# Five of eight experts in two passes with at most 64 tokens, other buffer counts, and a branch

## The chip, the cores and the metric

The kernel runs on one core of a Trainium2 chip. The metric is the device time of one execution in microseconds (us); the time shown is the median of several runs. The engines of the core work beside one another, each in its own order, and wait for one another by semaphores: TensorE (PE for its matmuls, PEld for its weight loads), VectorE (DVE), ScalarE (ACT), GpSimd (POOL) and SyncE (SP), which here issues the transfers from memory.

## The reference

Two layers over 256 tokens of 2048 float32 values. The even layer mixes by pooling and stick-breaking attention and then has a dense SwiGLU network of width 5632; the odd layer mixes by a gated unit and then sends each token to two of eight experts:

```python
DN_ALPHA = (2.0 * DEPTH) ** 0.25

def moe_swiglu(x, w_router, w_gu, w_down):
    logits = jnp.dot(xt, w_router, preferred_element_type=jnp.float32)
    top_vals, top_idx = lax.top_k(logits, TOP_K)                # 2 of 8
    top_w = jax.nn.softmax(top_vals, axis=-1)
    gates = jnp.sum(jax.nn.one_hot(top_idx, N_EXPERTS) * top_w[..., None], axis=1)
    y = jnp.zeros(xt.shape, jnp.float32)
    for e in range(N_EXPERTS):
        y = y + gates[:, e:e + 1] * swiglu(xt, w_gu[e], w_down[e])
    return y

def swiglu(x, w_gu, w_down):
    gate, up = jnp.split(x @ w_gu, 2, axis=-1)                  # 2048 -> 2 x 1408
    return (jax.nn.silu(gate) * up) @ w_down                    # 1408 -> 2048

h = layer_norm(DN_ALPHA * h + mixed @ odd_w_out, odd_ln1_g, odd_ln1_b)
h = layer_norm(DN_ALPHA * h + moe_swiglu(h, odd_router, odd_moe_w_gu, odd_moe_w_down), odd_ln2_g, odd_ln2_b)
```

## The kernel before

Stages, by the trace: the even mixer and its output projection to about 311 us, the dense network to 1047 us (11 column blocks, gate and up, then down), the odd mixer, its projection and the router to about 1340 us, eight experts to 2154.5 us, the final normalisation and output to 2174.2 us.

Products of float32 values are made from two parts each. A value is rounded to a shorter type (`fp32r`), which is its high part, and the remainder is what the rounding lost. `mm3` (lines 117 to 119) adds three products to one accumulator: high times high, high times the weights' remainder, remainder times the weights' high part.

All weights come by `load` (lines 97 to 110). A load brings PIECE = 4 row chunks of 128 x 512 (1 MB; 0.75 MB for narrower column blocks) into a buffer `raw` on SyncE's queue (line 106), ScalarE casts it to the high part `wh` (line 107), VectorE subtracts to get the remainder `wl` (line 108). There are five `raw` buffers and four pairs of `wh` and `wl`. A `raw` buffer is free for the next transfer when its split is done, a pair when the last matmul that reads it is. Before the experts, every block of loaded weights serves two token tiles of 128; the loop over pieces goes through both tiles.

An expert works on its own tokens only. `gather` compares each token's place in the expert's list with the numbers 1 to 128 (VectorE, line 819), which gives a one-hot matrix `Dt` for each token tile; a product with the tokens (line 837) brings up to 128 tokens into the columns of `xe`, high part and remainder, for two experts in one go. `slots` (line 848) turns `Dt` and reads the gates. `expert_up` makes gate and up in three column blocks (512, 512 and 384), each from four loads of four chunks, and the SwiGLU, whose product is transposed (line 181) and split. `expert_down` runs through four blocks of 512 columns of three loads (4, 4 and 3 chunks), scales by the gate and scatters back with `Dt` (lines 900 and 901), and adds to `h` (line 234). An expert is 24 loads of 1 MB and 12 of 0.75 MB. In the down part of experts 1, 3 and 5 the next pair is gathered, a quarter in each block.

If an expert has more than 128 tokens, a loop at the end (lines 728 to 751) runs all experts again for the rest; it stands behind a branch on the value `most`, and isn't run with these inputs.

The order of the instructions within each engine is found ahead of time by a planner, from its own estimates of durations; both arms of a branch are planned as units of their own. There is no barrier at the entry of an arm. At its end every engine waits for its own work, SyncE for all its transfers to land, before it jumps on.

## Time and profile before

| | |
|---|---|
| median of 3 runs | 2174.91 us (2174.14 to 2175.73) |
| the profiled execution: time, span | 2175.96 us, 2174.2 us |
| mean granted TensorE clock | 0.994 |
| PE busy | 2140.0 us (98%) |
| PEld busy | 1781.5 us (82%) |
| DVE busy | 1456.7 us (67%) |
| ACT busy | 1146.6 us (53%) |
| POOL busy | 1.6 us |
| DMA | mean 247 GB/s, 537.80 MB |
| end of experts 0 to 7 | 1458.8, 1562.4, 1658.4, 1762.8, 1859.5, 1963.2, 2059.3, 2154.5 us |

Busy times are of the whole span; the stages differ, so they have to be read by stretches. The experts' ends are those of their last scatter (line 901). Line numbers are those of the kernel before. The rows of a view of windows give, for a stretch (us from the start), its length, the busy us and the count of instructions of PE, PEld, DVE, ACT and POOL, the mean granted clock as a share of full speed (PEclk), the mean busy share of the 16 DMA engines, and the GB/s moved. A row of a group of instructions gives line, engine, operation, the tile written and those read, and their shapes; x is a count. "issue" and engine names with a q (SPq, DVEq) are the sequencer of that engine: what it spends waiting, loading registers or branching.

### The profile page before, as it was taken

Reading aid. Unit: us, or ns where it says so; the run is one execution under the profiler, and the core shown is the slowest. Engines: PE = TensorE matmul, PEld = TensorE weight load, DVE = VectorE, ACT = ScalarE, POOL = GpSimd, SP = SyncE. Lnnn points to the kernel's source line nnn. Section 1 sums busy time; section 2 is a strip of 40 time slices with the busy share of each in tenths; the row PEclk is TensorE's granted clock in tenths of the full one; section 3 lists DMA queues with packets and bytes.
Section 4 is the critical chain, followed back from the end, with each engine's and each line's share of the span. In section 5 each row is a group of like instructions: output and inputs, shape, how many; then the busy total and the mean of one; then the engine's idle time right before and its main releaser. Section 6 shows DMA issues by size and latency. Waiting matters only on the chain.

```text
span 2174.2 us, 24450 instructions
## 1 busy us (share of the span) xinstructions
PE 2140.0 (98%) x9955; PEld 1781.5 (82%) x9956; DVE 1456.7 (67%) x1225; ACT 1146.6 (53%) x962; POOL 1.6 (0%) x6
## 2 busy tenths in 40 slices
PE   9999999999999999999999999999999999999996
PEld 7888888888888888888788887888888888888884
DVE  5443566554454644556676546898889888888988
ACT  5444355343333433343644335766766767676764
POOL 0000000000000000000000000000000000000000
PEclk9999999999999999999999999999999999999998
DMA  8544645555454554545544643899989999998995
GB/s 347 217 147 145 233 180 208 211 194 191 157 215 172 213 189 169 204 169 218 213 182 166 235 155 117 320 352 357 340 331 367 347 336 342 346 352 322 371 351 213
DMA packets 82198, 537.80 MB, mean 247 GB/s; under 512 B 9504, under 2 KB 10656, under 8 KB 28192
## 3 DMA queue, kind: packets, MB, share of 16 engines
q1 hardware_dynamic: 82080, 536.18, 66.3%
q8 instruction: 80, 1.31, 0.2%
q14 instruction: 38, 0.31, 0.0%
HBM read 534.04 MB, written 2.10 MB: 247 GB/s over the span
## 4 chain that ended last, share of the span: by engine, by line
PE 93%; DVE 3%; ACT 2%; DMA 1%; issue 0%; SPq 0%; DVEq 0%; ACTq 0%
PE acc L118 29%; PE acc L119 28%; PE acc L117 28%; PE ps L181 2%; DVE wl L108 1%; PE ps L837 1%; ACT wh L107 1%; PE ps L900 1%; DMA raw<-in_odd_moe_down_dram 1%; DMA raw<-in_even_w_in_dram 1%; PE ps L901 1%; ACT lnT L259 0%; PE ps L575 0%; PE acc L135 0%; PE acc L629 0%
## 5 line engine op out<-in xcount | busy, mean ns | idle before, releaser
L108 DVE TENSOR_TENSOR wl<-raw,wh 128x2048 fp32r<-128x2048 f32 (+2 forms) x519 | 1121.3, 2178 | 391.5 <-ACT wh L107 390.8
L107 ACT CAST wh<-raw 128x2048 fp32r<-128x2048 f32 (+2 forms) x519 | 935.4, 1824 | 442.1 <-PE acc L119 399.3
L118 PE MATMUL acc<-wl,xh 128*128 128x512 f32 x928 | 363.3, 392 | 1.1 <-DVE wl L108 1.1
L117 PE MATMUL acc<-wh,xh 128*128 128x512 f32 x928 | 361.8, 390 | 0.1
L119 PE MATMUL acc<-wh,xl 128*128 128x512 f32 x928 | 361.6, 390 | 0.0
L118 PE MATMUL acc<-wl,xe 128*128 128x512 f32 (+1 forms) x752 | 280.7, 373 | 0.1
L119 PE MATMUL acc<-wh,xe 128*128 128x512 f32 (+1 forms) x752 | 279.4, 372 | 0.0
L117 PE MATMUL acc<-wh,xe 128*128 128x512 f32 (+1 forms) x752 | 278.6, 371 | 0.5 <-ACT wh L107 0.5
L118 PE MATMUL acc<-wl,hTh 128*128 128x512 f32 x704 | 277.3, 394 | 1.1 <-DVE wl L108 1.0
L119 PE MATMUL acc<-wh,hTl 128*128 128x512 f32 x704 | 276.1, 392 | 0.0
L117 PE MATMUL acc<-wh,hTh 128*128 128x512 f32 x704 | 274.8, 391 | 0.0
L118 PEld LDWEIGHTS acc<-wl,xh 128*128 128x128 f32 x928 | 174.4, 188 | 37.0 <-DVE wl L108 1.5
L117 PEld LDWEIGHTS acc<-wh,xh 128*128 128x128 f32 x928 | 174.2, 188 | 37.1 <-ACT xh L174 0.5
L119 PEld LDWEIGHTS acc<-wh,xl 128*128 128x128 f32 x928 | 174.4, 188 | 35.7 <-DVE xl L175 0.2
L118 PEld LDWEIGHTS acc<-wl,xe 128*128 128x128 f32 x752 | 141.2, 188 | 21.2 <-DVE wl L108 1.8
L117 PEld LDWEIGHTS acc<-wh,xe 128*128 128x128 f32 x752 | 141.2, 188 | 20.7 <-ACT wh L107 0.8
L118 PEld LDWEIGHTS acc<-wl,hTh 128*128 128x128 f32 x704 | 132.3, 188 | 30.3 <-DVE wl L108 3.5
L119 PEld LDWEIGHTS acc<-wh,xe 128*128 128x128 f32 x752 | 141.3, 188 | 19.0
L117 PEld LDWEIGHTS acc<-wh,hTh 128*128 128x128 f32 x704 | 132.3, 188 | 28.3
L119 PEld LDWEIGHTS acc<-wh,hTl 128*128 128x128 f32 x704 | 132.4, 188 | 26.4
L174 ACT CAST hTh<-ps 128x512 fp32r<-128x512 f32 (+1 forms) x46 | 26.2, 569 | 180.4 <-PE ps L181 180.4
L117 PE MATMUL acc<-wh,x0h 128*128 128x512 f32 x256 | 104.1, 409 | 2.5 <-ACT wh L107 2.5
(201 smaller groups left out, 1820.0 us busy)
## 6 DMA issues: line engine op xcount, KB each, us to landing
raw<-in_odd_moe_gu_dram SPq DMA_DIRECT2D x128, 1024.0 KB, 6.9
raw<-in_even_ffn_gu_dram SPq DMA_DIRECT2D x88, 1024.0 KB, 4.8
raw<-in_odd_moe_down_dram SPq DMA_DIRECT2D x64, 1024.0 KB, 7.0
raw<-in_odd_moe_gu_dram SPq DMA_DIRECT2D x64, 768.0 KB, 6.1
raw<-in_even_ffn_down_dram SPq DMA_DIRECT2D x44, 1024.0 KB, 4.8
raw<-in_odd_w_in_dram SPq DMA_DIRECT2D x32, 1024.0 KB, 4.8
raw<-in_even_w_in_dram SPq DMA_DIRECT2D x30, 1024.0 KB, 5.0
raw<-in_odd_moe_down_dram SPq DMA_DIRECT2D x32, 768.0 KB, 6.8
```

Source lines behind the costliest of these rows:

```text
L107: nc.scalar.copy(wh, raw)
L108: self.wl_ins = nc.vector.tensor_tensor(wl, raw, wh.bitcast(F32), ALU.subtract)
L117: mm(acc, xh, wh, start=first, stop=False)
L118: mm(acc, xh, wl, start=False, stop=False)
L119: mm(acc, xl, wh, start=False, stop=last)
L174: self.nc.scalar.copy(hi, src)
L181: self.nc.tensor.transpose(ps[:, j * P:(j + 1) * P], src[:, j * P:(j + 1) * P], self.ident)
L837: mm(o, xtok[t, c // 8][part][:, cs], Dt[t].rearrange("p a b -> p (a b)"), start=j == 0 and t == 0, stop=t == 1, skip_group_check=True)
L900: nc.tensor.matmul(ps, DT[:, t, :], yh, start=True, stop=False)
L901: nc.tensor.matmul(ps, DT[:, t, :], yl, start=False, stop=True)
```

## The change

The eight experts are no longer all alike and no longer in the order 0 to 7.

- Expert 0 runs as before, but its tokens are gathered alone. While it runs, a new function `order` sorts the other seven by whether they have more than SLIM = 64 tokens: those with more come first. The sort is 23 small operations of VectorE, and the seven expert numbers are loaded into registers of SyncE, so that weights are addressed by a register.
- The first FATS = 2 of the sorted seven run as before, in three passes with up to 128 tokens ("fat" experts). For them the next pair is gathered in expert 0's down part.
- The last five stand behind a branch on `full`, the count of experts among the seven with more than 64 tokens. If at most two have more, the new arm runs them as "slim" experts. If not, the other arm runs them as before.
- A slim expert holds at most 64 tokens. `gather_slim` puts the tokens' high parts into columns 0 to 63 of a 128-column operand and their remainders into columns 64 to 127. One matmul with the weights' high part then makes two of the three products, and a second one with the weights' remainder a third (and a fourth, remainder times remainder): two passes instead of three. `fold` adds rows 64 to 127 of the accumulator to rows 0 to 63: ScalarE copies the accumulator, and a product with a shifted identity is added to it. In the down part the hidden values stand in the same way, and the scatter, with `Dt` in both halves, does the adding.
- In the slim arm two experts are gathered at its start, three more in the second one's down part. The first EARLY = 2 loads of the first of the five experts are made ahead of the branch and used by either arm.
- There are seven `raw` buffers instead of five, and three split pairs instead of four, in the whole kernel.
- In the last down projection of the dense network the order changes from all four column blocks of token tile 0, then all of tile 1, to block 0 of tile 0 and of tile 1, then blocks 1 to 3 of tile 0, then blocks 1 to 3 of tile 1.
- The final scales and biases (G, B) are still loaded behind all experts' loads in the program, which is now behind the branch.

```diff
+SLIM = 64
+EARLY = 2
+FATS = 2
+REST = NEXP - 1
...
-        nc.sync.dma_start(raw, src)
+        self.issued = nc.sync.dma_start(raw, src)
...
-                order = [(t, n) for t in range(NT) for n in range(NCB)] if last else \
-                        [(t, n) for n in range(NCB) for t in range(NT)]
+                order = [(t, n) for n in range(NCB) for t in range(NT)]
+                if last:
+                    order.sort(key=lambda k: k[1] > 0 and 1 + k[0])
...
-                    if last and (t, n) in ((1, 0), (1, NCB - 1)):
+                    if last and (t, n) in ((1, 1), (1, NCB - 1)):
...
+        self.fold = pm.tile([P, P], F32R, tag="fold", name="fold", bufs=1)
+        nc.gpsimd.memset(self.fold[:, SLIM:].bitcast(F32), 0.0)
+        nc.gpsimd.tensor_copy(self.fold[:, :SLIM], self.ident[:, SLIM:])
...
-        gat = self.gather(xtok, [pos1[t][:, 0:2] for t in range(NT)], gg, 0, 0)
+        gat = self.gather(xtok, [pos1[t][:, 0:1] for t in range(NT)], gg, 0, 0, num=1)
...
+        many = pm.tile([P, REST], F32, tag="many", name="many", bufs=1)
+        nc.vector.tensor_scalar(many, cnt[:, 1:NEXP], float(SLIM), None, ALU.is_gt)
+        ids, posP, full = [], [], pm.tile([P, 1], I32, tag="full", name="full", bufs=1)
+        def gather(k, num):
+            return self.gather(xtok, [posP[t][:, k:k + num] for t in range(NT)], gg, NEXP + k, 0, num=num)
+        def gather_slim(k, num):
+            return self.gather_slim(xtok, [posP[t][:, k:k + num] for t in range(NT)], num)
+        def prepare():
+            order = self.order(many, pos1, gates, gate_cols, posP, full)
+            ins, v = nc.values_load_multi_w_load_instructions(
+                order[0:1, :], engines=[mybir.EngineType.SP], min_val=1, max_val=REST)
+            self.after(ins[0], self.issued)
+            ids.extend(v)
+        hT = self.expert_up(0, gat, 0, first, prepare)
+        gat[4]()
+        cur, gat = gat, gather(0, FATS)
+        gat[4]()
+        self.expert_down(0, cur, 0, hT, True, None, gat[3])
+        for p in range(FATS):
+            hT = self.expert_up(ids[p], gat, p)
+            self.expert_down(ids[p], gat, p, hT, False, None)
+        full_v = nc.values_load(full[0:1, 0:1], min_val=0, max_val=REST)
+        src = i["odd_moe_gu"][ids[FATS], 0]
+        early = [self.load(src[k]) for k in range(EARLY)]
+        with tc.If(full_v < FATS + 1) as slim:
+            at = 0
+            A, step = gather_slim(FATS, 2)
+            for q in range(4):
+                step(q)
+            for k in range(FATS, REST):
+                ahead = partial(gather_slim, k + 1, REST - k - 1) if k == FATS + 1 else None
+                nxt = self.slim_expert(ids[k], k - FATS - at, A, gg, NEXP + k, fstats if k == REST - 1 else None,
+                                       early if k == FATS else None, ahead)
+                if nxt is not None:
+                    A, at = nxt, 2
+        with slim.Else():
+            for k in range(FATS, REST, 2):
+                num = min(2, REST - k)
+                gat = gather(k, num)
                 gat[4]()
-            step = None
-            if e % 2 and e + 1 < NEXP:
-                gat = self.gather(xtok, [pos1[t][:, e + 1:e + 3] for t in range(NT)], gg, e + 1, 0)
-                gat[4]()
-                step = gat[3]
-            self.expert_down(e, cur, e % 2, hT, e == 0, fstats if e == NEXP - 1 else None, step)
+                for q in range(4):
+                    gat[3](q)
+                for p in range(num):
+                    hT = self.expert_up(ids[k + p], gat, p, early=None if k + p > FATS else early)
+                    self.expert_down(ids[k + p], gat, p, hT, False, fstats if k + p == REST - 1 else None)
...
+    def order(self, hv, pos1, gates, gate_cols, posP, full):
...
+        self.after(v.tensor_reduce(H, hv, AX.X, ALU.add), self.wl_ins)
+        v.tensor_copy(full, H)
+        v.tensor_tensor(sq, rows(hv), square(C_LOWER), ALU.mult)
+        v.tensor_reduce(rank, sq, AX.X, ALU.add)
+        v.scalar_tensor_tensor(a, e7, H, rank, ALU.add, ALU.subtract)
+        v.tensor_tensor(b, rank, a, ALU.subtract)
+        v.tensor_tensor(b, b, hv, ALU.mult)
+        v.tensor_tensor(a, a, b, ALU.add)
+        v.tensor_tensor(perm, rows(a), square(C_PLACE), ALU.is_equal)
+        v.tensor_scalar(b, e7, 1.0, None, ALU.add)
+        v.tensor_tensor(sq, perm, rows(b), ALU.mult)
+        v.tensor_reduce(b, sq, AX.X, ALU.add)
+        v.tensor_copy(ids, b)
+        for t in range(NT):
+            g = tile("gateP", [P, R], bufs=2)
+            x = tile("posP", [P, R], bufs=2)
+            for dst, src in ((x, pos1[t]), (g, gates[t])):
+                v.tensor_tensor(sq, perm, rows(src[:, 1:NEXP]), ALU.mult)
+                v.tensor_reduce(dst, sq, AX.X, ALU.add)
+            gate_cols(t, g, 2 * NEXP, R)
+            posP.append(x)
+        return ids
...
+    def gather_slim(self, xtok, pos, num):
+        nc, pm = self.nc, self.pm
+        mm = nc.tensor.matmul
+        slots = self.iota1[:, :SLIM].unsqueeze(1).to_broadcast([P, 2, SLIM])
+        d4 = []
+        for t in range(NT):
+            d = pm.tile([P, num, 2, SLIM], F32R, tag="Dt", name="d4", bufs=2)
+            for p in range(num):
+                nc.vector.tensor_scalar(d[:, p], slots, pos[t][:, p:p + 1], None, ALU.is_equal)
+            d4.append(d)
+        A, units = {}, {}
+        per = 4 // num if num < 3 else 1
+        w = num * SLIM
+        hold = 8 // num if num < 3 else 2
+        def quarter(q):
+            for c in range(4 * q, 4 * q + 4, per):
+                if c % hold == 0:
+                    units[0] = self.unit("xs", shape=[P, hold, num, 2, SLIM])
+                ps = self.ps()
+                for j in range(per):
+                    cs = slice((c + j) % 8 * P, ((c + j) % 8 + 1) * P)
+                    for part in range(2):
+                        o = ps[:, (2 * j + part) * w:(2 * j + part + 1) * w]
+                        for t in range(NT):
+                            mm(o, xtok[t, (c + j) // 8][part][:, cs], d4[t][:, :, 0, :],
+                               start=j == 0 and part == 0 and t == 0, stop=t == 1, skip_group_check=True)
+                for j in range(per):
+                    u = units[0][:, (c + j) % hold]
+                    nc.scalar.copy(u, ps[:, 2 * j * w:2 * (j + 1) * w].rearrange("p (a e s) -> p e a s", a=2, e=num))
+                    A[c + j] = u
+        return (A, d4), quarter
...
+    def slim_expert(self, e, p, gat, gg, col, stats, early, ahead):
+        nc, i, pm = self.nc, self.i, self.pm
+        mm = nc.tensor.matmul
+        A, d4 = gat
+        def two(groups, lhs, w):
+            acc = self.acc()
+            n, k0 = sum(g[2] for g in groups), 0
+            for wh, wl, kc in groups:
+                for j in range(kc):
+                    mm(acc[:, :w], lhs(k0 + j), wh[:, j, :], start=k0 + j == 0, stop=False)
+                    mm(acc[:, :w], lhs(k0 + j), wl[:, j, :], start=False, stop=k0 + j == n - 1)
+                k0 += kc
+            return acc
+        def fold(acc, w):
+            c = self.pln.tile([P, CB], F32R, tag="lnT", name="low")
+            nc.scalar.copy(c[:, :w], acc[:, :w])
+            mm(acc[:, :w], self.fold, c[:, :w], start=False, stop=True, skip_group_check=True)
+        hT = []
+        for b, w in enumerate(EXP_W):
+            accs = [two(self.up_loads(e, b, u, early),
+                        lambda k: A[k][:, p], w) for u in range(2)]
+            for acc in accs:
+                fold(acc, w)
+            nch = w // P
+            s = self.pln.tile([P, CB], F32, tag="lnT", name="silu")
+            nc.scalar.activation(s[:, :w], accs[0][:, :w], AF.Silu)
+            nc.vector.tensor_tensor(s[:, :w], s[:, :w], accs[1][:, :w], ALU.mult)
+            pv = self.transpose4(s, nch)[:, :w].rearrange("p (c t) -> p c t", c=nch)[:, :, :SLIM]
+            h = pm.tile([P, 4, 2, SLIM], F32R, tag="hTh", name="hT2", bufs=3)
+            nc.scalar.copy(h[:, :nch, 0, :], pv)
+            nc.vector.tensor_tensor(h[:, :nch, 1, :], pv, h[:, :nch, 0, :].bitcast(F32), ALU.subtract)
+            hT.append(h)
+        DT, gs = self.slots([d4[t][:, p] for t in range(NT)], gg, col)
+        nxt, step = (None, None) if ahead is None else ahead()
+        for n in range(NCB):
+            if step is not None:
+                step(n)
+            acc = two(self.down_loads(e, n), lambda k: hT[k // 4][:, k % 4], CB)
+            self.scatter(acc, DT, gs, n, False, stats)
+        return nxt
...
-                groups = self.loads(i["odd_moe_gu"][e, b * 2 + u] if b < 2 else i["odd_moe_gu2"][e, u], w)
-                accs.append(self.block(groups, lhs, 0, w))
+                accs.append(self.block(self.up_loads(e, b, u, early), lhs, 0, w))
             hT.append(self.swiglu(pm, accs[0], accs[1], w, w // P, "m"))
+            if then is not None and b == 0:
+                then()
...
+    def up_loads(self, e, b, u, early):
+        src = i["odd_moe_gu"][e, b * 2 + u] if b < 2 else i["odd_moe_gu2"][e, u]
+        if early is None or b or u:
+            return self.loads(src, EXP_W[b])
+        return early + [self.load(src[k]) for k in range(EARLY, src.shape[0])]
...
-        self.praw = e(self.pool("raw", 5))
-        self.pw = e(self.pool("w", 4))
+        self.praw = e(self.pool("raw", 7))
+        self.pw = e(self.pool("w", 3))
```

## Rows read from the trace of the kernel before

**Rows 1.** Windows by stage: length, busy (count) of five engines, PEclk, DMA share, GB/s.

```profile
0.00:1340.00 1340.00, 1332.34 (x6081) 1093.65 (x6083) 742.97 (x681) 568.23 (x506) 1.61 (x6) 1.00 0.53 196
1459.00:2154.50 695.50, 692.90 (x3318) 590.04 (x3317) 595.91 (x396) 489.07 (x373) 0.00 (x0) 1.00 0.92 343
```

**Rows 2.** Windows, the same columns: expert 2, and the last five experts.

```profile
1562.40:1658.40 96.00, 96.00 (x451) 82.10 (x451) 83.83 (x54) 66.75 (x46) 0.00 (x0) 1.00 0.93 349
1658.40:2154.50 496.10, 493.52 (x2357) 419.54 (x2357) 424.87 (x282) 346.55 (x263) 0.00 (x0) 1.00 0.91 342
```

**Rows 3.** Waits of SyncE's queue: waiting line, releaser; us in all, times, longest.

```profile
SPq L106 <- DVE wl L108: 1785.4, 494, 20.5
```

**Rows 4.** Timeline of PE: start, duration, engine, line, operation, shapes, type, count.

```profile
1499.74 0.39 PE L118 MATMUL acc<-wl,xe 128*128 128x512 f32 x1
1499.97 0.39 PE L119 MATMUL acc<-wh,xe 128*128 128x512 f32 x1
1500.20 0.33 PE L118 MATMUL acc<-wl,xe 128*128 128x384 f32 x1
1500.37 0.34 PE L119 MATMUL acc<-wh,xe 128*128 128x384 f32 x1
...
1551.78 1.10 PE L837 MATMUL ps<-Dt,xtl 128*128 128x256 f32 x8
```

**Rows 5.** Groups by form, 1460 to 2060 us: busy, mean ns, idle before.

```profile
L108 DVE TENSOR_TENSOR wl<-raw,wh 128x2048 fp32r<-128x2048 f32 x144 | 325.5, 2288 | 51.0 <-ACT wh L107 50.8
L108 DVE TENSOR_TENSOR wl<-raw,wh 128x1536 fp32r<-128x1536 f32 x72 | 124.3, 1754 | 13.6 <-ACT wh L107 13.2
```

**Rows 6.** Timeline: a cast and its split, idle time before in brackets.

```profile
257.77 1.91 ACT L107 CAST wh<-raw 128x2048 fp32r<-128x2048 f32 x1 [11.64 <-PE acc L119]
259.71 2.29 DVE L108 TENSOR_TENSOR wl<-raw,wh 128x2048 fp32r<-128x2048 f32 x1 [3.25 <-ACT wh L107]
```

**Rows 7.** Windows in which the DMA queue was full.

```profile
20.00:50.00 30.00, 29.79 (x131) 24.35 (x131) 16.84 (x11) 15.13 (x14) 0.00 (x0) 1.00 1.00 410
1370.00:1390.00 20.00, 20.00 (x92) 16.56 (x91) 18.65 (x11) 15.22 (x10) 0.00 (x0) 1.00 1.01 403
```

**Rows 8.** Instructions of lines 728 and 729: ns (least/median/most), us from the start.

```profile
L728 SPq TENSOR_LOAD <-most x1: 472/472/472, 1347.6 to 1347.6; - x1
L728 PEldq TENSOR_LOAD <-most x1: 488/488/488, 2154.4 to 2154.4; - x1
L729 PEldq COMPARE_BRANCH  x1: 3370/3370/3370, 2155.0 to 2155.0; - x1
L729 DVEq COMPARE_BRANCH  x1: 72/72/72, 2169.0 to 2169.0; - x1
```

**Rows 9.** Timeline of PE: the last scatter of expert 2.

```profile
1658.21 0.62 PE L901 MATMUL ps<-yl,DT 128*128 128x512 f32 x2
```

**Rows 10.** Timeline: last scatter, the add behind it; four comparisons.

```profile
1346.40 0.87 DVE L819 TENSOR_SCALAR Dt<-c,pos 128x128 fp32r<-128x128 f32 x4
...
2154.20 0.73 PE L901 MATMUL ps<-yl,DT 128*128 128x512 f32 x2
2154.74 1.28 DVE L234 TENSOR_TENSOR h<-h,ps 128x512 f32<-128x512 f32 x2 [0.59 <-PE ps L901]
```

**Rows 11.** DMA issues: the final scales; count, KB each, us to landing.

```profile
gb<-in_odd_ln_b_dram SPq DMA_DIRECT2D x4, 512.0 KB, 6.8
```

**Rows 12.** Windows around the fall of the granted clock.

```profile
1340.00:1345.00 5.00, 3.82 (x28) 2.93 (x26) 4.24 (x23) 3.68 (x8) 0.00 (x0) 1.00 0.01 2
1345.00:1350.00 5.00, 3.06 (x14) 2.91 (x14) 4.22 (x18) 2.19 (x5) 0.00 (x0) 0.52 0.00 0
```

**Rows 13.** Waits of PEld: waiting operation, releaser; us in all, times, longest.

```profile
PEld ps L181 <- DVE silu L528: 6.0, 22, 0.3
```

**Rows 14.** Timeline of PE: the dense network's start, tiles 0 and 1.

```profile
311.02 0.39 PE L134 MATMUL acc<-wh,xh 128*128 128x512 f32 x1
...
319.56 0.66 PE L181 MATMUL ps<-c,h 128*128 128x128 f32 x4
```

More of the change, by code (lines that the diff above doesn't have):

```diff
@@ L845, in slots @@
             for p in range(num):
[L846 to L854 removed]
+                DT, gs = self.slots([Dt[t][:, p, :] for t in range(NT)], gg, e + p)
                 DTs.append(DT)
@@ L861, in expert_up @@
+    def expert_up(self, e, gat, p, first=None, then=None, early=None):
+        pm = self.pm
         xe = gat[0]
```

94 lines of the change are left out of this document (60 added, 34 removed).

## Prediction

> **What bounds the kernel now.** I read the busy times by stage first. Up to 1340 us, and again from 1459 to 2154.5 us, TensorE is busy for all but a few us of the stretch, VectorE for 55% and 86% of it, ScalarE for 42% and 70%, the DMA engines for 0.53 and 0.92 of their time [rows 1]. So TensorE is the bound nearly everywhere, and it alone of the engines is full; but in the experts the DMA engines and VectorE stand close behind it. An expert that gathers nothing for the next pair takes 96.0 us, all of it TensorE; the last five take 496.1 us, in which VectorE works 424.9 us and the DMA engines 0.91 of the time [rows 2]. Those two numbers say what the change can win at most: with TensorE out of the way, VectorE leaves 85.0 us an expert against 99.2.
>
> Then the loop that feeds an expert. A load is issued when VectorE has split the load five before it (SyncE waits for the split at line 108 for 1785 us in all, 494 times) [rows 3]; so the raw buffers are a closed loop of transfer, cast, split.
>
> **Which arm runs.** The reference's router, evaluated on the reference's inputs, gives the eight experts 42, 47, 57, 114, 53, 34, 109 and 56 tokens. Of experts 1 to 7 two have more than 64. `full` is 2, under FATS + 1, and the slim arm runs: experts 0, 3 and 6 in three passes, then 1, 2, 4, 5, 7 in two.
>
> **The slim expert, priced per engine.** TensorE: the third pass goes, 64 matmuls of 512 columns and 32 of 384 in the up part, 44 of 512 in the down part. From start to start they take 0.23 and 0.17 us [rows 4]: 64 x 0.23 + 32 x 0.17 + 44 x 0.23 = 30.3 us. Six folds of at most 0.23 us come in, 1.4 us. 96.0 - 30.3 + 1.4 = 67 us; two gathers of 64 matmuls at 0.12 us (eight of them, twice as wide, take 1.10 with the last one's tail [rows 4]) add 15 / 5 = 3: 70 us. TensorE is no longer the bound.
> VectorE: the splits stay, 24 x 2.29 + 12 x 1.75 = 76 us of its 85.0 [rows 2, 5]; half a column block less to split in the hidden part and a few small operations more leave it at 85.
> ScalarE: 346.6 / 5 = 69 us [rows 2], plus six copies for the folds, each a quarter of the columns of a cast of 1.91 us [rows 6], 0.5: 72.
> DMA: 34.6 MB an expert (24 loads of 1 MB and 12 of 0.75). The stretches in which the queue is full move 403 and 410 GB/s [rows 7], which gives 84 to 86 us; by the share of the experts as they run now, 0.91 x 99.2, it is 90 us [rows 2]. I take it to lie between, since seven raw buffers keep two more loads in flight.
> So VectorE at 85 and DMA at 84 to 90 are what is late next. Neither will be full: VectorE must meet a cast before each split, and sits behind the adds and the two-operand products that wait for TensorE. In the one stretch where VectorE drove this loop it was busy 18.65 of 20 us, 93% [rows 7]. 85 / 0.93 = 91 us an expert, 2.53 us a load. From 87 (98% busy) to 95.
>
> **The branch.** No row shows a fall-through into an arm. Every engine loads the flag into a register (0.47 and 0.49 us in two of them) and branches; the branch to a far target held TensorE 3.37 us and VectorE 0.07 [rows 8]. For the entry I take 1.3 us (0.6 to 3.9), nearest to VectorE's. Queued behind it on each engine is all of the arm; SyncE passes early, as it has only to load the flag, and goes on filling raw buffers, so transfers don't stop. From the last scatter of the second fat expert, which stands here where expert 2 ends at 1658.8 [rows 9]: two adds to h end 1.1 us later [rows 10]; branch 1.3; four comparisons for the slots 0.9 [rows 10]; 64 gather matmuls at 0.12, 7.5; eight matmuls of the first load 1.8; then a pair is free, and its cast ends 1.9 us later [rows 6]: 14.5 us after the scatter VectorE starts its fourth split of the arm (two were split ahead of the branch, one went into the third pair). 177 splits remain: 177 x 91 / 36 = 447.4; and about 5 us for the last split, matmuls and scatter. 14.5 + 447.4 + 5 = 466.9 against 496.1: **29.2 us gained**.
>
> **What is paid for it.**
> Leaving the arm is a jump over the other one: 0.1 to 3.4 us [rows 8], on VectorE's way to the final normalisation; 2.5 taken, as the other arm is long like the loop that TensorE jumped. The last scales and biases (G, B) were loaded during the last expert; now SyncE issues them only when it has left the arm, that is, when every load has landed. A jump and a landing of 6.8 us [rows 11] stand against the last cast, split, matmuls, scatter and VectorE's own jump, some 12 us: nothing, and up to 3 if that cover is short.
> `order`: 23 small operations at some 0.2 us [rows 10], 4.6 us of VectorE in expert 0, and seven register loads at 0.47 plus a check on SyncE [rows 8], two loads late. The split pairs hold about 8 us of TensorE's work, which hides most of it: 2 (0 to 5).
> The clock: after a stretch in which TensorE was busy 3.82 of 5 us with small matmuls, the granted clock was 0.52 for the next 5 us, nearly all at the lower of its two levels, 1.2 GHz [rows 12]. The entry of the arm looks alike: 1.5 (0 to 3.4).
> **Three pairs instead of four**, everywhere. Before the experts a block of 16 chunks is four loads, used by token tile 0 and then by tile 1. With three pairs the fourth load can only be split when tile 1 has used the first one, so the planner must run tile 1 on the first three groups ahead of tile 0's fourth. The refill takes 1.91 + 2.29 and gaps, 4.4 us from free to split [rows 6]; two groups (24 matmuls at 0.23) cover 5.4 us. It fits, but is now drawn up to the edge: the planner puts the fourth group where it believes the split done. Its belief can be off: the transposes that it places behind a swiglu waited 6.0 us in 22 places, 0.27 each [rows 13]. 45 such blocks at 0.27 would be 12 us; at nothing, 0. The feed-forward stage starts with tile 0 at 311.0 while tile 1's first transposes come at 319.6 [rows 14]; three groups of tile 0 end at about 319.2 instead of 322, so tile 1 is wanted before it is there; the same where the odd layer starts: 0 to 4 us each. The reordered last down projection loses one of four blocks of cover for tile 0's normalisation, which I cost at nothing beyond that. Together 7 (0 to 20).
> In the three fat experts a pair is used once: 2.7 us of TensorE against a refill of 4.4, so three pairs give one load per (2.7 + 4.4) / 3 = 2.4 us, under 2.7 but with little to spare when VectorE has adds and products in between, as it has in the down part: 3 (0 to 8).
> Two raw buffers more: nothing before the experts, where TensorE is full [rows 1].
>
> **Sum.** -29.2 + 2.5 + 2 + 1.5 + 7 + 3 = -13 on a span of 2174.2, 2161. The profiled run took 2175.96, the median is 2174.91, so a run lies about 1 us over its span: **2162 us**.
>
> **Rivals.**
> 1. The transfers don't speed up: whatever holds them at 349 GB/s in the 96.0 us expert [rows 2] isn't the number of buffers. Place: the five slim experts. 34.6 / 0.349 = 99 us an expert, 177 x 99 / 36 + 19.5 = 506 against 496.1: with the 16 paid, 2200. It decides from (496.1 - 16 - 19.5) x 36 / 177 = 93.7 us an expert upward, 369 GB/s: above that time the kernel is slower. For it: the share is 0.93 already at that rate. Against: 403 to 410 with the queue full. 0.12.
> A rule of the Trainium skill stands beside this rival: "DMA: Bandwidth & Descriptors", section Specifications, gives a core 358 GB/s of HBM. By it an expert would take 34.6 / 0.358 = 97 us and the sum would come to some 2190. The trace of before disagrees with it in the two stretches with the queue full, at 403 and 410 GB/s [rows 7].
> 2. Three pairs starve the first 1340 us: the planner covers the refill with one group, not two. 4.4 - 2.7 = 1.7 us in 45 blocks, 76 us: 2161 - 7 + 76 = 2230. From 20 us, 0.45 a block, it eats the gain. For it: the fourth group is drawn in as early as it can be. Against: 5.4 us of other work exist. 0.10.
> 3. Better: VectorE at 98% (87 us an expert, -20) and the early stages untouched (-10): 2130. 0.13.
> 4. The clock falls in the slim experts, where TensorE is busy some 77% in short pieces. At 0.5 its 70 us are 140, and 5 x 49 us are lost: 2410; it decides from a clock of 0.75. The rows show it only after small matmuls [rows 12]. 0.03.
> 5. The other arm runs, or the branch costs far more than 4 us: about 2200. The counts speak against it. 0.02.
> My forecast has 0.60, from 2142 to 2178. The range that leaves out no more than rivals 2, 4, 5 and the ends of 1 is 2130 to 2195. Of the forecast 0.47 lies under 2170.5 (0.2% is about what a measurement can tell), 0.10 within, 0.03 above 2179.3; with rival 3 and rivals 1, 2, 4 and 5: faster 0.60, same 0.12, slower 0.28. (0.02 of rival 1 falls within.)
>
> **What would show it.** Slim experts of about 91 us, VectorE 93% busy, DMA at 380 GB/s or more, TensorE 77%; some 14 us between the last fat scatter and VectorE's steady splitting; TensorE idle for 0 to 0.3 us per block before 1340 us, waiting for the split or its cast. Experts over 94 us with DMA at a share of 0.97 or more and VectorE under 90% would prove rival 1; TensorE waits of a us and more at line 118 before 1340 us, rival 2.

## The result and the profile after

The changed kernel takes 2947.59 us (median of 4 runs, 2945.92 to 2949.51) against 2175.32 us for the kernel before in the same comparison: 1.355 times as long (95% interval 1.353 to 1.358). The forecast was 2162 us with a range of 2130 to 2195. The profiled execution has a span of 2947.8 us and a mean granted clock of 0.81.

The page's slices show at once where the time is (40 slices of 73.7 us; busy tenths of TensorE, VectorE and ScalarE, the granted clock in tenths, the DMA engines' busy tenths):

```profile
PE   9999999999999999998999975665665665565564
...
DVE  4445564554555567556888823333333333333334
ACT  4453533343333353434777632223332322222222
...
PEclk9999999999999999998999955556666555555555
DMA  8455455555455554553889933443443444344341
```

From slice 24 on everything is half idle: TensorE, VectorE, ScalarE and the DMA engines alike, and the granted clock is at 0.5 to 0.6. No engine is the bound there. The stages in windows (stretch, length, busy us (count) of PE, PEld, DVE, ACT, POOL, clock, DMA share, GB/s):

```profile
0.00:1350.00 1350.00, 1334.38 (x6014) 1084.42 (x6015) 724.21 (x634) 556.85 (x495) 2.50 (x8) 0.99 0.54 194
1693.40:2925.70 1232.30, 750.99 (x1704) 477.12 (x1703) 435.71 (x290) 363.90 (x295) 0.00 (x0) 0.57 0.39 136
```

The second row is the slim arm, from the last scatter of the third expert to that of the eighth. It answers the second row of [rows 2]: 1232.3 us where the last five experts took 496.1. VectorE works 435.7 us in it, about as long as before (424.9), TensorE 751 us at a clock of 0.57. Ahead of the arm the kernel is 34.6 us late (1693.4 against 1658.8 us, by the end of the scatter), of which 28 us are there by the first row's end (by the splits around it, four at a time). After it the end is 22.1 us away, where it was 19.3. So 736 of the 773.6 us of difference in span lie in the arm.

What holds the arm is in the waits (us in all, times, longest, from 1693 to 2926 us) and in one load's round:

```profile
ACT wh L118 <- PE acc L1012: 784.9, 175, 6.9
DVE wl L119 <- ACT wh L118: 724.2, 178, 15.0
PEld acc L1012 <- ACT wh L118: 370.3, 176, 2.3
PEld acc L1013 <- DVE wl L119: 301.2, 174, 2.1
```

```profile
2320.26 1.47 ACT L118 CAST wh<-raw 128x1536 fp32r<-128x1536 f32 x1 [4.17 <-PE acc L1012]
2321.76 1.76 DVE L119 TENSOR_TENSOR wl<-raw,wh 128x1536 fp32r<-128x1536 f32 x1 [3.88 <-ACT wh L118]
...
2321.78 0.69 PE L1012 MATMUL acc<-wh,xs 128*128 128x384 f32 x1 [1.24 <-ACT wh L118]
...
2323.57 0.69 PE L1013 MATMUL acc<-wl,xs 128*128 128x384 f32 x1 [1.10 <-DVE wl L119]
...
2325.89 1.47 ACT L118 CAST wh<-raw 128x1536 fp32r<-128x1536 f32 x1 [4.17 <-PE acc L1012]
```

Read from top to bottom: the cast ends, and the first matmul of this same load can go; the split ends, and the second can; and only when the load's last matmul with the high part is through (the releaser of the cast, line 1012) does ScalarE begin the next cast, 5.63 us after the last one began. Cast, split and matmuls take turns, 175 times for the 178 loads that are split in the arm. The list of waits has none for a transfer: raw data lie ready and wait. A pipeline of three pairs doesn't look like that; a single pair does.

The built program says the same. These are the places of the tile `wh` (byte offset: number of loads) ahead of the branch and in the slim arm:

```
changed kernel, ahead of the branch   66528: 114   82912: 114   74720: 113
changed kernel, slim arm                                        74720: 178
EARLY = 1, slim arm                                82912: 90    74720: 89
EARLY = 0, slim arm                   66528: 60    82912: 60    74720: 60
```

The two loads made ahead of the branch stand in the pairs at 66528 and 82912. They are read inside the branch, and in the slim arm no other load is put into their places, although their last matmul comes some us after its start. (Whether that takes a read in both arms or in one was not tried.) The arm turns over on the one pair that is left. The `raw` buffers are not held: their casts and splits stand ahead of the branch, and all seven turn over in the arm.

### The profile page after: what moved, and what is told of

Its sections match the earlier page's. It is cut to its first block, busy times and chain, and to the rows that moved or that the text cites. A ratio compares the mean times of both kernels' runs of the same rounds, so it can differ in the third digit from the quotient of the medians.

```text
span 2947.8 us, 23727 instructions
## 1 busy us (share of the span) xinstructions
PE 2416.8 (82%) x9286; PEld 1837.9 (62%) x9286; DVE 1466.0 (50%) x1249; ACT 1161.7 (39%) x994; POOL 2.5 (0%) x8
## 4 chain that ended last, share of the span: by engine, by line
PE 72%; DVE 15%; ACT 11%; issue 1%; DMA 0%; SPq 0%; DVEq 0%
PE acc L128 17%; PE acc L129 17%; PE acc L130 17%; DVE wl L119 13%; ACT wh L118 11%; PE acc L1013 9%; PE acc L1012 7%; PE ps L192 1%; PE ps L992 1%; PE ps L1104 1%; PE ps L894 0%; PE ps L1103 0%; PE ps L587 0%; PE ps L459 0%; ACT lnT L270 0%
## 5 line engine op out<-in xcount | busy, mean ns | idle before, releaser
L1012 PE MATMUL acc<-wh,xs 128*128 128x512 f32 (+1 forms) x480 | 293.1, 611 | 170.7 <-ACT wh L118 170.7
L1013 PE MATMUL acc<-wl,xs 128*128 128x512 f32 (+1 forms) x480 | 300.7, 626 | 155.4 <-DVE wl L119 155.4
L1012 PEld LDWEIGHTS acc<-wh,xs 128*128 128x128 f32 x480 | 149.2, 311 | 260.9 <-ACT wh L118 245.7
L1013 PEld LDWEIGHTS acc<-wl,xs 128*128 128x128 f32 x480 | 151.7, 316 | 228.2 <-DVE wl L119 205.7
L1012 PE MATMUL acc<-wh,hT 128*128 128x512 f32 x220 | 138.4, 629 | 85.7 <-ACT wh L118 85.7
L1013 PE MATMUL acc<-wl,hT 128*128 128x512 f32 x220 | 139.6, 635 | 67.0 <-DVE wl L119 67.0
L129 PE MATMUL acc<-wl,hTh 128*128 128x512 f32 x484 | 190.1, 393 | 0.5 <-DVE wl L119 0.5
L130 PE MATMUL acc<-wh,hTl 128*128 128x512 f32 x484 | 190.3, 393 | 0.0
L128 PE MATMUL acc<-wh,hTh 128*128 128x512 f32 x484 | 189.3, 391 | 0.0
L1013 PEld LDWEIGHTS acc<-wl,hT 128*128 128x128 f32 x220 | 65.7, 299 | 109.3 <-DVE wl L119 95.5
L128 PE MATMUL acc<-wh,x0h 128*128 128x512 f32 x256 | 102.7, 408 | 2.3 <-ACT wh L118 2.3
```

Source lines behind the costliest of these rows:

```text
L128: mm(acc, xh, wh, start=first, stop=False)
L129: mm(acc, xh, wl, start=False, stop=False)
L130: mm(acc, xl, wh, start=False, stop=last)
L1012: mm(acc[:, :w], lhs(k0 + j), wh[:, j, :], start=k0 + j == 0, stop=False)
L1013: mm(acc[:, :w], lhs(k0 + j), wl[:, j, :], start=False, stop=k0 + j == n - 1)
```

## The experiments

All medians are of their own comparison, in which the kernel before took 2175.1 to 2175.9 us; the first row has its time as it stood ahead of the prediction. "Arm" is the time from the last scatter of the third expert to that of the eighth in the profiled execution (the last five experts, where there is no arm), and "pairs" the pairs that turn over in the arm.

| kernel | raw, pairs in all | pairs in the arm | third expert ends | arm | us | ratio to before (interval) |
|---|---|---|---|---|---|---|
| before | 5, 4 | 4 | 1658.8 | 496.1 | 2174.91 | |
| changed | 7, 3 | 1 | 1693.4 | 1232.3 | 2947.59 | 1.3551 (1.3528 to 1.3575) |
| EARLY = 1 | 7, 3 | 2 | 1690.8 | 561.8 | 2277.41 | 1.0478 (1.0461 to 1.0496) |
| EARLY = 0 | 7, 3 | 3 | 1690.2 | 501.3 | 2216.81 | 1.0198 (1.0181 to 1.0215) |
| five pairs | 3, 5 | 3 | 1704.2 | 587.4 | 2316.63 | 1.0669 (1.0641 to 1.0698) |
| before with the new pools | 7, 3 | 3 | 1690.9 | 496.3 | 2209.48 | 1.0163 (1.0146 to 1.0180) |
| filled | 7, 3 | 1 | 1694.1 | 1217.7 | 2936.17 | 1.3496 (1.3469 to 1.3523) |
| filled inside blocks | 7, 3 | 1 | 1693.1 | 1110.3 | 2826.64 | 1.2991 (1.2970 to 1.3013) |
| EARLY = 0, old pools | 5, 4 | 4 | 1658.1 | 507.1 | 2188.79 | 1.0055 (1.0038 to 1.0072) |
| EARLY = 0, no branch | 7, 3 | 3 | 1693.2 | 493.4 | 2199.90 | 1.0111 (1.0094 to 1.0128) |
| EARLY = 0, no fold | 7, 3 | 3 | 1690.3 | 501.4 | 2218.88 | 1.0202 (1.0185 to 1.0219) |
| late fold, old pools | 5, 4 | 4 | 1658.4 | 473.6 | 2156.35 | 0.9913 (0.9899 to 0.9926) |
| late fold and late scaling | 5, 4 | 4 | 1660.3 | 480.0 | 2164.30 | 0.9957 (0.9943 to 0.9970) |
| late fold, new pools | 7, 3 | 3 | 1692.3 | 459.2 | 2174.63 | 0.9995 (0.9985 to 1.0005) |

### Are the pairs taken?

No load ahead of the branch:

```diff
-EARLY = 2
+EARLY = 0
```

> The changed kernel with EARLY = 0: no load of the slim arm is made ahead of the branch, nothing else differs. Theory 1 (taken pairs: the two pairs filled ahead of the branch belong to both arms, so they stay taken through the whole arm, and the arm runs on the one pair that is left): all three pairs turn over in the arm, the five slim experts take 455 to 500 us instead of 1232, the clock stays near full in them, the run 2150 to 2215 us. Theory 2 (clock: TensorE's short pieces of work in a slim expert bring its clock down to about 0.57 by themselves, whatever the buffers): the clock stays at 0.5 to 0.6 in the arm and the run at 2400 us or more. Theory 3 (the order within an arm puts cast, split and matmuls one behind the other, whatever the buffers): within 20 us of 2948.

2216.81 us: 731 of the 772 us of loss are gone with this one number, the clock over the arm is 0.97, and the arm takes 501.3 us. Theories 2 and 3 fall. The run is 2 us over the upper end that theory 1 gave, as is the arm by 1 us, since it is still as long as before's; that is taken up below.

```profile
1690.20:2191.50 501.30, 409.87 (x1704) 300.48 (x1703) 427.29 (x292) 358.07 (x297) 0.00 (x0) 0.97 0.89 335
```

One load ahead (`EARLY = 1`):

> The changed kernel with EARLY = 1: one load ahead of the branch. Theory 1: two pairs are left, a load takes half of (cast 1.9 + split 2.3 + gaps 0.2 + matmuls 1.9 at full clock or 3.7 at half): 3.2 to 4.1 us, 112 to 146 us an expert, the run between 2270 and 2450. Theory 2: the clock as with EARLY = 2, about 0.57, and the run over 2400. Theory 3: within 20 us of 2948.

2277.41 us, at theory 1's lower end: two pairs cost 60 us over three, one pair costs 731. The step from two to one is so large, as I read it, because with two pairs the cast and split of one load still lie beside the matmuls of the other, and the clock holds (0.96 over the arm).

The same EARLY = 2, but more pairs:

```diff
-        self.praw = e(self.pool("raw", 7))
-        self.pw = e(self.pool("w", 3))
+        self.praw = e(self.pool("raw", 3))
+        self.pw = e(self.pool("w", 5))
```

> The changed kernel with EARLY = 2 and five pairs and three raw buffers (the same bytes as seven and three). Theory 1: three pairs are left in the arm, so the slim experts run as in the kernel with EARLY = 0, if three raw buffers keep the transfers going: 2130 to 2250 us; the first 1350 us, 28 us longer than before with three pairs, come back to within 10 us of before. Theories 2 and 3: the arm stays at 2.4 times of before, and the run over 2400.

2316.63 us, 67 over the upper end. That the loss is not tied to EARLY itself is shown (the arm takes 587 us, not 1232), and the first stages are back (1.3 us late at split 240, where the kernels with three pairs are 32 to 34); but I was wrong that three raw buffers keep the transfers going. The experts ahead of the arm are slowed as well (the third ends at 1704.2 us). In the arm ScalarE now waits for landings, a wait that the arm with EARLY = 0 and seven buffers does not show:

```profile
ACT wh L118 <- DMA raw<-in_odd_moe_gu_dram: 91.0, 73, 3.4
ACT wh L118 <- DMA raw<-in_odd_moe_down_dram: 42.7, 31, 4.0
```

### What three pairs cost elsewhere

The kernel before, with `self.pool("raw", 7)`, `self.pool("w", 3)` and the changed order of the last down projection, nothing else.

> The kernel before with seven raw buffers and three pairs, and the last down projection in the changed order (with three pairs the old order needs four blocks at once), no slim experts and no branch around them. If three pairs alone cost what the trace shows ahead of the slim arm (35 us to the end of the third expert), the run is 2174 + 28 to 60 = 2200 to 2235 us. If that delay comes from the sort and the single gather, 2175 to 2190.

2209.48 us, 34 over before: the whole delay ahead of the arm. Its last five experts take 496.3 us, as before. With five raw buffers and four pairs, and the new order of the last down projection kept, the delay is gone (EARLY = 0, old pools: third expert at 1658.1 us). So the order costs nothing beside four pairs, the sort next to nothing, and the delay comes with the pools of seven and three; that it is the pairs is seen in what waits. Where it sits is seen in what TensorE's weight loads wait for up to 1350 us, first in the kernel before, then in the changed one:

```profile
PEld acc L117 <- ACT wh L107: 3.5, 2, 2.9
```

```profile
PEld acc L128 <- ACT wh L118: 18.7, 42, 2.8
```

and at the start of the dense network, in the changed kernel's windows, where tile 1 is wanted before its normalisation is done:

```profile
310.00:315.00 5.00, 2.54 (x14) 1.97 (x13) 4.83 (x11) 2.89 (x3) 0.00 (x0) 0.93 0.12 23
315.00:320.00 5.00, 4.24 (x18) 3.25 (x17) 4.77 (x6) 4.97 (x14) 0.00 (x0) 0.73 0.67 220
...
325.00:330.00 5.00, 2.27 (x13) 1.29 (x11) 2.81 (x4) 3.49 (x8) 0.00 (x0) 1.00 0.50 169
330.00:335.00 5.00, 4.56 (x14) 3.40 (x15) 1.39 (x2) 3.94 (x9) 0.00 (x0) 0.66 0.89 354
```

A short stall of TensorE there is paid twice, since the next few us run at a lower clock: 0.73 behind the stretch with 2.54 busy us of 5, 0.66 behind the one with 2.27. By the order of the splits, the changed kernel is 4.5 us late at split 48 and 14.9 us at split 56, around this start. The odd layer's start adds a smaller step: in the means of four splits, 19.9 us late at split 172 and 26.0 at split 192.

### How much of the one pair's cost is the clock?

Matmuls that nobody reads, between the loads of a slim expert, so that TensorE is busy while it waits:

```diff
             for wh, wl, kc in groups:
+                ps = self.ps()
+                for _ in range(4 * kc):
+                    x = mm(ps, one[:, :P], one, start=True, stop=True)
+                    self.after(x, self.tail)
                 for j in range(kc):
```

> The changed kernel (EARLY = 2, one pair left in the arm), with matmuls that nobody reads (512 columns, 16 or 12 of them) between the matmuls of one load and the next in the slim experts, so that TensorE works while it waits for the cast and the split. If the lower clock in the arm comes from TensorE's idle time between loads, the clock goes to 1.0 and a load of 1 MB takes cast 1.91 + split 2.29 + matmuls 2.0 = 6.2 us, the others 4.8: 206 us an expert instead of 246, the run 2730 to 2800 us; what is left above 2217 is then the one pair alone. If the clock is not what lengthens the loads beyond that chain, 2940 or longer.

2936.17 us: missed, and inconclusive by its total. The mean clock came up to 0.93 in the arm, and inside a block the loads ran as expected, 5.97 us apart; but the first fills of a block ran behind fold and transposes and ahead of the block's first matmul, and gave the gain back (12.3 us from one split to the next there, against 8.1 in the changed kernel). So once more, with the fills left out ahead of each block's first load (`if k0:`):

> The changed kernel (EARLY = 2, one pair) with the matmuls that nobody reads, but none ahead of a block's first load, where those of the first such kernel held up the fold, the transposes and the first cast. In the first one a 1 MB load inside a block took 5.97 us at full clock against 7.24 us in the changed kernel at half clock, a 0.75 MB load 4.86 against 5.64. If the clock costs what these steps say, 16 x 1.27 + 10 x 0.78 = 28 us an expert come back: the run 2948 - 110 to 150 = 2798 to 2838 us. If the clock is no cost of its own, 2935 to 2950.

2826.64 us, 121 us less, as expected. The splits inside a block (VectorE's timeline), in the changed kernel and with the fills:

```profile
2209.43 2.29 DVE L119 TENSOR_TENSOR wl<-raw,wh 128x2048 fp32r<-128x2048 f32 x1 [4.95 <-ACT wh L118]
2216.67 2.29 DVE L119 TENSOR_TENSOR wl<-raw,wh 128x2048 fp32r<-128x2048 f32 x1 [4.95 <-ACT wh L118]
```

```profile
2213.86 2.29 DVE L119 TENSOR_TENSOR wl<-raw,wh 128x2048 fp32r<-128x2048 f32 x1 [3.75 <-ACT wh L118]
2219.83 2.29 DVE L119 TENSOR_TENSOR wl<-raw,wh 128x2048 fp32r<-128x2048 f32 x1 [3.67 <-ACT wh L118]
```

7.24 against 5.97 us a load, 5.64 against 4.86 for the smaller ones. Over all 36 loads of an expert that makes 24 x 1.27 + 12 x 0.78 = 40 us, about 200 us for the five (an estimate: only 26 of the 36 were filled). The rest, by this estimate over 500 us, is the turn-taking itself. The clock is an effect of the one pair here, not the cause: with two or three pairs it stays up (0.96 and 0.97 over the arm).

### Why the arm is no faster than before

EARLY = 0 leaves an arm of 501.3 us where I had forecast 466.9. Six runs went to that.

> EARLY = 0 with the pools of before, five raw buffers and four pairs. If the 33 us ahead of the experts come from three pairs and nothing else, they are gone (within 8 us of before at the end of expert 0's first load), and the run is 2217 - 33 = 2184 us or less; the arm with four pairs 470 to 500 us where three pairs took 501. If seven raw buffers are what lets the transfers reach 0.96 to 0.98 of the engines' time in the slim experts, five lengthen the arm by 10 us or more, and the run is 2190 to 2215.

2188.79 us, between the two forecasts: the 33 us came back as the first said, and with four pairs and five raw buffers the arm is 5.8 us longer than with three and seven, not shorter.

The slim arm without the test of `full` and without the second arm:

> EARLY = 0, the slim arm as straight code: the value of full is not looked at and there is no second arm. If entry and exit cost what the prediction put down (1.3 + 2.5, and about 14 us until VectorE splits steadily), 2217 - 4 to 18 = 2199 to 2213 us. If the slim experts are bound by the branch in no way, 2214 to 2220.

2199.90 us, 17 less, near the lower end. The profiled execution is the longest of the four (2207.65 us, the others 2199.48 to 2200.22), so the trace shows only 8 of the 17 us. In it the first slim expert takes 99.9 instead of 109.1 us, and the end comes 19.3 instead of 22.5 us after the last scatter; against that the third expert ends 3.0 us later, and the second slim expert takes 1.5 us more. The branch instructions themselves are small on entry (0.04 to 0.09 us on each engine). Without the branch the gather begins 2.7 us ahead of the third expert's end, with it 1.7 us behind. But the slow gather is not the branch's alone. Without the branch, in this execution, two gather matmuls first take 0.22 us together, from start to start, and some us later 0.43:

```profile
1690.70 0.39 PE L980 MATMUL ps<-d,xtl 128*128 128x128 f32 x2
1690.92 0.39 PE L980 MATMUL ps<-d,xth 128*128 128x128 f32 x2
...
1696.06 0.63 PE L980 MATMUL ps<-d,xth 128*128 128x128 f32 x2
1696.49 0.63 PE L980 MATMUL ps<-d,xtl 128*128 128x128 f32 x2
```

What the other 9 us of the 17 are, no trace shows. Behind the branch, the windows of the late-fold kernel, whose third expert ends at 1658.4 us, show the clock:

```profile
1655.00:1660.00 5.00, 2.54 (x10) 1.17 (x8) 2.59 (x7) 0.69 (x1) 0.00 (x0) 1.00 0.44 185
1660.00:1665.00 5.00, 5.00 (x25) 4.86 (x26) 0.24 (x2) 2.23 (x5) 0.00 (x0) 0.57 0.01 3
1665.00:1670.00 5.00, 5.00 (x25) 5.00 (x25) 2.98 (x2) 4.58 (x9) 0.00 (x0) 0.50 0.18 26
1670.00:1675.00 5.00, 5.00 (x21) 4.71 (x22) 4.34 (x3) 5.00 (x8) 0.00 (x0) 0.50 0.85 333
```

After the stretch in which TensorE was busy 2.54 of 5 us, the granted clock is at its lower level (1.2 GHz) for some 15 us, and a gather matmul takes 0.21 us.

Then the pace. In the kernel with EARLY = 0 the slim experts that gather nothing differ: the third takes 85.8 us, the fourth 96.9, with the same work. ScalarE's and VectorE's timelines at a block's end, third expert:

```profile
1912.53 1.91 ACT L118 CAST wh<-raw 128x2048 fp32r<-128x2048 f32 x1 [1.49 <-PE acc L1012]
1914.33 0.58 ACT L1019 CAST low<-acc 128x512 fp32r<-128x512 f32 x1
1914.81 1.92 ACT L118 CAST wh<-raw 128x2048 fp32r<-128x2048 f32 x1
...
1908.49 17.70 DVE L119 TENSOR_TENSOR wl<-raw,wh 128x2048 fp32r<-128x2048 f32 x8
```

and fourth expert:

```profile
1994.96 1.90 ACT L118 CAST wh<-raw 128x2048 fp32r<-128x2048 f32 x1 [0.46 <-PE acc L1012]
2000.79 0.59 ACT L1019 CAST low<-acc 128x512 fp32r<-128x512 f32 x1 [3.93 <-PE acc L1013]
2001.27 5.51 ACT L118 CAST wh<-raw 128x2048 fp32r<-128x2048 f32 x3
...
1994.33 6.69 DVE L119 TENSOR_TENSOR wl<-raw,wh 128x2048 fp32r<-128x2048 f32 x3
2003.21 8.90 DVE L119 TENSOR_TENSOR wl<-raw,wh 128x2048 fp32r<-128x2048 f32 x4 [2.19 <-ACT wh L118]
```

In the third, the fold's copy comes after more casts of the next block, finds TensorE done and waits for nothing; VectorE splits eight loads without a gap. In the fourth the planner put it further ahead. ScalarE stands 3.93 us until the block's last matmul, the casts that could run stand behind it, and VectorE, which sets the pace, is idle for 2.19 us.

Without the fold:

> EARLY = 0 without the fold: rows 64 to 127 of the up accumulators are not added to rows 0 to 63, so the remainders' product is left out. Theory 4 (the fold's copy stands in ScalarE's queue and waits for the block's last matmul, 57 us in 26 places, with the casts of the next loads behind it, so that VectorE starves): the run 2217 - 15 to 35 = 2182 to 2202 us. Rival (the transfers, at 0.96 to 0.98 of the engines' time in two of the five, set the pace): 2210 to 2219.

2218.88 us: no change, in the range that I had given to the rival, the transfers. Theory 4 in this form falls: with the fold gone, the SwiGLU's activation and the hidden values' cast stand and wait in its place. First the copy's wait in the kernel with EARLY = 0, then theirs:

```profile
ACT low L1019 <- PE acc L1013: 57.2, 27, 3.9
```

```profile
ACT silu L1028 <- PE acc L1013: 35.2, 13, 3.9
ACT hT L1032 <- PE ps L192: 24.8, 14, 3.7
```

So it may be not the copy but the place in the queue. The next kernel tests that against the transfers; it keeps the fold and fixes its place, on five raw buffers and four pairs; to do so, a block's loads are written ahead of the fold of the block before:

```diff
+            groups = self.up_loads(e, (m + 1) // 2, (m + 1) % 2, early) if m < 5 else self.down_loads(e, 0)
+            fold(acc, w, self.casts[-len(groups):][2])
...
-            nc.scalar.copy(c[:, :w], acc[:, :w])
+            self.after(nc.scalar.copy(c[:, :w], acc[:, :w]), fence)
```

> EARLY = 0, five raw buffers, four pairs, and one order fixed: in the slim experts the fold's copy on ScalarE comes behind the casts of the next block's first three loads (the loads of a block are written ahead of the fold of the block before). Theory 5 (the pace of a slim expert hangs on how many casts stand ahead of the copy that waits for a block's last matmul: with three, as in the third slim expert of the kernel with EARLY = 0, VectorE splits on without a gap and the expert takes 86 us; with one, as in the fourth, VectorE waits 2.2 us a block and it takes 97): all slim experts that gather nothing take 85 to 90 us, the arm 465 to 485 us instead of 507, the run 2147 to 2168 us, faster than before. Rival (the transfers set the pace, at 0.96 and more of the engines' time): the arm stays over 495 us, the run over 2177. If other copies simply take the fold's place, as without the fold, also over 2177.

2156.35 us, 0.991 of before (0.990 to 0.993): 19 us under before, a small gain but clear of the noise, and the rival falls. The arm is 473.6 us, 33.5 less than with the planner's own place; the experts that gather nothing take 84.5, 91.2 and 92.6 us, the last two a little over what I expected. In its waits over the arm the fold's copy no longer waits for a matmul. Waits for landings have grown, from 14.1 us in the kernel with the planner's own place and the same pools to 39.0:

```profile
ACT wh L118 <- DMA raw<-in_odd_moe_down_dram: 7.5, 9, 1.5
ACT wh L118 <- DMA raw<-in_odd_moe_gu_dram: 6.6, 9, 1.4
```

```profile
DVE wl L120 <- ACT wh L118: 37.2, 50, 5.7
ACT wh L118 <- DMA raw<-in_odd_moe_gu_dram: 30.0, 38, 2.8
...
ACT wh L118 <- DMA raw<-in_odd_moe_down_dram: 9.0, 14, 1.3
```

> As the kernel with the late fold copy, and in the down part of the slim experts the scaling yh on ScalarE comes behind the casts of the next block's first two loads instead of one. Theory 5: VectorE's 1.04 us gaps in the down blocks go (two or three an expert): 5 to 12 us less than with the late fold alone. Rival (transfers): within 3 us of it. If scatter and adds are now late: 0 to 10 us longer.

2164.30 us, 8 longer: missed. ScalarE now waits 30.6 us in 7 places for VectorE's adds before it can scale, against 9.1 in 2. VectorE waits 4.8 us less for casts, but its adds wait 18.8 us for the scatter instead of 5.7. Why the scaling has to wait for those adds was not tried apart; there is one buffer each for `yh` and `yl`.

Last, the pools of the change with the late fold:

> The kernel with the late fold copy, with seven raw buffers and three pairs instead of five and four. Three pairs cost 33 us ahead of the experts, as in the other kernels with three. In the arm: if two more raw buffers speed the transfers up, as the prediction had it (with five, ScalarE waits 39 us for landings there), the arm is 5 to 35 us shorter than 474, the run 2155 to 2185 us; if three pairs hold back cast and split as much as five raw buffers hold back the transfers, 474 +- 5, 2184 to 2195; if three pairs are the tighter, 2195 to 2215.

2174.63 us, no difference from before (0.9995, 0.9985 to 1.0005), in the first of the three forecasts. The arm takes 459.2 us, 14.4 less than with five raw buffers and four pairs, and its waits for landings are gone:

```profile
1692.30:2151.50 459.20, 404.71 (x1703) 297.04 (x1703) 424.88 (x292) 359.09 (x297) 0.00 (x0) 0.98 0.93 366
```

So in the arm two raw buffers are worth more than a pair, and ahead of it a pair is worth 32 to 34 us: each of the two settings is right for one half of the kernel.

## Why the prediction was wrong

**The step that failed** is in the paragraph on the branch: "eight matmuls of the first load 1.8; then a pair is free, and its cast ends 1.9 us later", and all that follows from it. The text counted the pairs at the branch ("two were split ahead of the branch, one went into the third pair") and took for granted that a pair comes back with its last matmul, as it does in straight code. Inside the arm a pair that was filled ahead of the branch does not come back. The runs showed in its place one pair for all of the arm: a load of 1 MB every 7.24 us inside a block where 2.53 were forecast, 242 to 252 us an expert instead of 91, an arm of 1232.3 us instead of 466.9. Nothing in the rows of before could show that; but the diff did show tiles made ahead of the branch and read in both arms, and the count of three minus two was all that was missing. None of the rivals held it: rival 2 looked for starving pairs ahead of 1340 us, rival 4 for the clock alone. A loop of one pair could have been priced from the rows used: cast 1.91, split 2.29 [rows 6], seven matmuls at 0.23 behind it [rows 4], gaps: some 6 us a load at full clock (an estimate), which the 5.97 us of the filled kernel bear out; 24 x 6 + 12 x 4.8 = 202 us an expert where the sum had 91, and the lower clock comes on top.

**The clock** (rival 4, 0.03) came in, at 0.57, but because of the one pair. As a rival of its own, short pieces and TensorE busy for some 80% of the arm, it did not come true: 0.97 over the arm with three pairs.

The other steps can be judged in the kernels with EARLY = 0:

- **The slim expert's pace**, 91 us: within reach, but not with the instruction order of the change. With the late fold and the pools of the change, the experts that gather nothing take 83.0, 86.9 and 90.5 us, and the arm 459.2 against the forecast 466.9; VectorE works 85.0 us an expert in it, as forecast, TensorE 80.9 instead of 70. With the planner's own order these experts take 85.8, 96.9 and 102.7 us, and the arm 501.3: the step that priced ScalarE at 72 us, with six copies for the folds at 0.5 each, took the copies' busy time, and not that each waits for TensorE with casts queued behind it. This is 42 us in the arm (501.3 against 459.2, one edit, in which the loads of a block are also written earlier).
- **Rival 1**, transfers stuck at 349 GB/s: wrong. The third slim expert with EARLY = 0 moves 389 GB/s, the arm with the late fold 366 in the mean. That two more raw buffers help the arm is right, 14 us against a fourth pair. The rule that I had set beside the rival, from the Trainium skill ("DMA: Bandwidth & Descriptors", section Specifications, 358 GB/s to a core), is not a limit that these traces show.
- **Three pairs ahead of the experts**, 7 (0 to 20): under-sized, 32 to 34 us. The term for the 45 blocks, at most 12 us, measured 18.7 us of weight loads waiting for casts in 42 places, 3.5 before; the start of the dense network, put at 0 to 4 us, cost about 10, that of the odd layer, also 0 to 4, about 6. The rival that starved every block at 1.7 us (76 us in all) was too large; but the delay is over the 20 us from which it was said to eat the gain, so this term alone would have turned the forecast from faster to slower.
- **Fat experts**, 3 (0 to 8): nothing. In the kernel before with the new pools all eight experts run as before on three pairs; it is 33.3 us late at split 240, nine loads into the experts, and 32.1 at the third expert's end, and its last five take 496.3 us against 496.1. **The sort**, 2 (0 to 5): about right. With the single gather and the two early loads it comes to 2.5 us, the difference between the changed kernel and that one at the third expert's end (1693.4 and 1690.9).
- **Entry**: VectorE's fourth split of the arm, from which it splits steadily, begins at 1709.2 us in the kernel with EARLY = 0, 19.0 us after the third expert's end; the forecast, with two loads made ahead, was 14.5 + 1.5 for the clock. The branch itself was taken too dear (1.3; under 0.1 on each engine), the slow clock in the gather too cheap: at 0.21 us, as in the late-fold kernel, instead of 0.12, 64 matmuls are 5.8 us longer, against the 1.5 put down.
- **Exit**: 2.5 forecast, 3.2 measured (22.5 against 19.3 us after the last scatter).

With the pair step put right, the forecast's terms and the measured size of the three pairs would have given about 2162 + 27 = 2189 for a kernel with EARLY = 0 and a good order; the measured one is 2174.63.

**Left open**: whether the order alone, or the earlier written loads with it, give the late fold its gain; why the second slim expert, which gathers three at once, takes 13 to 23 us more than the third with EARLY = 0 (either pools, without the branch, without the fold) and with the late fold (either pools), and 9 with the late scaling; and what 9 of the 17 us are that go with the branch.

## What to carry to other kernels

A buffer that is filled ahead of a branch and read in its arms is gone for the whole arm: before such a prefetch, count the buffers that still turn over inside; from three to two it cost 60 us here, from two to one 670. An evacuation that waits for TensorE must be priced by what stands behind it in its engine's queue, not by its own half microsecond; its place among the casts, with the loads written earlier, was worth 33 to 42 us here, and taking the operation away was worth nothing. When every engine goes half idle at once and the clock falls, look for a chain that takes turns on one buffer first, and for the clock afterwards.

## What the runs showed of the hardware

The fall of the granted clock is itself a term: the same chain of cast, split and matmuls ran at 7.24 us a load at a clock of about 0.57 and 5.97 us with TensorE kept busy by matmuls that nobody reads, 121 us in all for work that produces nothing. And in these traces a stall of a few us at a stage's start is followed by a stretch at the lower level: in the late-fold kernel most of 15 us behind the branch, where small gather matmuls took 0.21 us each; 0.11 us is what they took at first in the kernel without the branch, before they slowed to 0.21 there too.
